# Moving the samples' state products and two key products of a decoder trunk from VectorE to GpSimd

## The chip, the core and the metric

The kernel runs on one core of one Trainium2 chip. The metric is the time of one execution on the device in microseconds (us); less is better. The engines are named as the profile names them: PE is TensorE, DVE is VectorE, ACT is ScalarE, POOL is GpSimd, and SP is SyncE, which here issues nearly all the transfers.

## The reference

Two layers of a decoder trunk run for one prompt of 256 tokens (with 16 learned meta tokens ahead of it, 272 rows) and for 8 samples of one token each; both groups share the weights. Layer 0 is RWKV-7 time mixing with 64 heads of 64, layer 1 is windowed attention on a shared K/V. All arithmetic is float32. What matters here is layer 0:

```python
def rwkv7_step(S, inp):
    r, d, k, v, kk, b = inp
    sa = jnp.einsum('bhij,bhj->bhi', S, kk)
    S = S * d[:, :, None, :] - sa[..., None] * b[:, :, None, :] + v[..., None] * k[:, :, None, :]
    return S, jnp.einsum('bhij,bhj->bhi', S, r)
...
    kk = k_h * k_k.astype(f32).reshape(hn)
    kk = kk / jnp.maximum(jnp.sqrt(jnp.sum(kk * kk, axis=-1, keepdims=True)), 1e-12)
    k_h = k_h * (1.0 + (a_h - 1.0) * k_a.astype(f32).reshape(hn))
    b_h = kk * a_h
...
    y = y + jnp.sum(r_h * k_h * r_k.astype(f32), axis=-1, keepdims=True) * v_h
    y = y.reshape(B, T, WIDTH).astype(dt) * jax.nn.silu(z)
    return y @ w_out, S_fin.astype(S0.dtype), xn[:, -1]
```

For the samples `T` is 1 and the state `S` comes in from outside: 8 x 64 heads x 64 x 64 numbers. The last addition is called the bonus below.

## The kernel before

The activations lie transposed: 128 channels (two heads) on the partitions, 280 columns beside each other (272 prompt rows, then the 8 samples). A weight tile `raw_*` of 128 x 512 is loaded by SP, ACT casts it to `whi_*` (line 195), DVE subtracts to get `wlo_*` (line 197), and PE forms each product in three parts (lines 218 to 220: high by high, low by high, high by low). A weight tile feeds 12 such matmuls. This goes on from start to end, so PE always has such a product to do if its weights are split in time.

The span has three stages. Until about 140 us the input is normalised and the first projections run. From about 140 to 1240 us `phase_a` runs (this is where the change lies): PE's order is written by hand in `drive`, which walks through the large products in pieces of six matmuls (one piece is one *position*) and lets small streams put their work between the pieces. A stream is a Python generator: `yield 5` gives the word back for five positions, and `yield 5, f` waits beyond that until `f()` holds. So a number in a `yield` is a distance on PE, while ACT, DVE and POOL get what a list scheduler of the toolchain makes of the program; each engine then runs its own list in order. After 1240 us come the output projection, the attention layer and the final projection.

The streams that the change and the prediction touch:

- `preps`: `prep(u)` for 16 pairs of channel tiles (u is 0 to 15). It loads `kT` and `rT` (keys and receptance, 128 x 2 x 280), scales `kk`, forms the factor `km` on ACT (line 902), multiplies it into `kT` in place on DVE (line 904), forms `ta` (line 906) and the running sum of the decay (line 910). POOL gathers the samples' eight columns of six tensors into `sm` (line 932); PE turns `sm` around (line 935, tile `ps_sm`), and ACT copies it out (line 937). Then the bonus: `rk` is r times r_k times k (line 945), split into `rklhi` (ACT) and `rkllo` (DVE) like a weight, and summed over a head on PE (line 954, `ps_bo`); DVE multiplies the sum into `vT` (line 955). Buffers of `km` and of `rk` share the tag "sq", which has two.
- `main`: for pairs of u (o is 0 to 7), `solve(o)` and `chain(o)`, the recurrence over five blocks of rows. Ahead of a solve stands `substitute(o)`: four POOL instructions on 128 x 256 to 128 x 320 (lines 1064 to 1067: `Noff`, two `nd`, `N`), then a DVE transpose (`NL`, line 1069), 28 small dependent DVE instructions (lines 1075 and 1077), and the transposes `TN` and `TR` (lines 1081, 1082), on which PE's `ps_so` (line 1102) waits. In the chain's fifth block POOL clears `W` (line 1198). DVE's `X<-FS` (line 1227) lets PE's next block begin (line 1191).
- `group_norm(o)`: PE transposes (`ps_yt`, line 1275), DVE scales into the bonus tile `vT` (line 1276).
- `decodes`: `decode(g)` for four groups of samples' states, each in eight pieces `dS` of 128 x 512. DVE multiplies the piece by `kk` into `dT` and sums (lines 1313, 1314), then by `ddr` (d times r) and sums. `dS` and `dT` have one buffer each, so the next piece's load waits for the last reader. The flag `self.samples` is true only while a chain runs, and a piece is let in only then.

`late_gates` waits for `('d', 3)`, the end of the fourth group, and for the last chain.

Of the kernel before, what the change touches and what calls it, by code (L numbers as in the profile page):

```python
# [12 lines left out]
F32 = mybir.dt.float32  # L13
F32R = mybir.dt.float32r
I32 = mybir.dt.int32
AF = mybir.ActivationFunctionType
ALU = mybir.AluOpType
AX = mybir.AxisListType
# [7 lines left out]
L = NM + SEQ  # L26
NS = 8
N = L + NS
# [32 lines left out]
P_W0, P_A0, P_KK, P_KA, P_RK, P_GG, P_GB = 144, 176, 208, 256, 288, 320, 352  # L61
# [48 lines left out]
class Kernel:  # L110
# [747 lines left out]
    def prep(self, u):  # L858
        nc, rp, I = self.nc, self.rp, self.I
        V, A, G = nc.vector, nc.scalar, nc.gpsimd  # L860
        tt = V.tensor_tensor
        MU, AD, SU = ALU.mult, ALU.add, ALU.subtract
        dma = nc.sync.dma_start
        p0 = 2 * u
        b, sl = p0 // 4, slice(p0 % 4, p0 % 4 + 2)
        w = lambda n, bufs=1: rp.tile([128, 2, N], F32, tag=n, bufs=bufs, name=f"{n}{u}")
# [5 lines left out]
        hi = rp.tile([128, 544], F32R, tag="lhi", name=f"lhi_{u}")[:LR, :512]  # L872
# [17 lines left out]
        kT = w("kT", 2)  # L890
        dma(kT, self.kd[b][:, sl])
        rT = w("rT")
        dma(rT, self.rd[b][:, sl])

        kk = w("kk")
# [4 lines left out]
        for j in range(2):  # L900
            km = rp.tile([128, N], F32, tag="sq", bufs=2, name=f"km{j}_{u}")
            A.activation(km, a[:, j], AF.Identity, scale=self.par2[:, 64 + p0 + j:65 + p0 + j],
                         bias=self.par2[:, 96 + p0 + j:97 + p0 + j])
            tt(kT[:, j], kT[:, j], km, op=MU)
        A.activation(a, a, AF.Identity, scale=-0.5, bias=self.half[:, 1:2])
        tt(a, a, kk, op=MU)
        A.activation(cl, cl, AF.Identity, scale=0.5, bias=self.half[:, 0:1])

        for j in range(2):
# [28 lines left out]
        g, h0 = p0 // 8, (2 * p0) % 16  # L938
# [1 line left out]
            dma(self.vecd[g][:, :, h0 + 2 * j:h0 + 2 * j + 2].rearrange("v b h j -> (v b) (h j)"),  # L940
                sr[48 * j:48 * j + 48].rearrange("p h j -> p (h j)"))

        def rk_of(j):
            rk = rp.tile([128, L], F32, tag="sq", bufs=2, name=f"rk{j}_{u}")
            V.scalar_tensor_tensor(rk, rT[:, j, :L], self.pcol(P_RK, p0 + j), kT[:, j, :L], op0=MU, op1=MU)
            self.split(two[0][:, j], two[1][:, j], rk)
        two = [rp.tile([128, 2, L], F32R, tag=n, name=f"rk{n}{u}") for n in ("lhi", "llo")]
        for j in range(2):
            rk_of(j)
        for j in range(2):  # L950
            yield 5 - j if u > 1 else 3, self.pp_free
            ps = self.pp_bank(f"ps_bo{j}_{u}")
# [329 lines left out]
    def decode(self, g):  # L1282

        nc, rp, I, O = self.nc, self.rp, self.I, self.O
        V, A, G = nc.vector, nc.scalar, nc.gpsimd
        tt = V.tensor_tensor
        MU, AD = ALU.mult, ALU.add
        dma = nc.sync.dma_start
        ve = rp.tile([128, 6, 64], F32, tag="ve", name=f"ve{g}")
        dma(ve, self.vecd[g].rearrange("v b h j -> (b h) v j"))  # L1290
        kk, bn, kp, rr, vv, dd = (ve[:, i] for i in range(6))
        gb = rp.tile([128, 3, 64], F32, tag="gb", name=f"gb{g}")
        dma(gb, I['consts'][:, C_GB + 192 * g:C_GB + 192 * g + 192].rearrange("p (v j) -> p v j", v=3))
        y = rp.tile([128, 64], F32, tag="dy", name=f"dy{g}")
        sa = rp.tile([128, 64], F32, tag="dsa", name=f"dsa{g}")
        t = rp.tile([128, 64], F32, tag="dt2", name=f"dt2{g}")
        st = rp.tile([128, 8], F32, tag="dst", name=f"dst{g}")

        dr = rp.tile([128, 64], F32, tag="ddr", name=f"ddr{g}")
        tt(dr, dd, rr, op=MU)  # L1300
        NI = 8
        rowb = lambda a: a.unsqueeze(1).to_broadcast((128, NI, 64))
        for q in range(64 // NI):
            if q:
                yield 3
            S = rp.tile([128, NI, 64], F32, tag="dS", bufs=1, name=f"dS{g}_{q}")
            T = rp.tile([128, NI, 64], F32, tag="dT", bufs=1, name=f"dT{g}_{q}")
            iq = slice(NI * q, NI * q + NI)
            dma(S.rearrange("p i j -> p (i j)"),
                I['state_wkv'][g, q])  # L1310
            yield 5 if g < 3 else 4, lambda: self.samples
            for w, o in ((kk, sa), (dr, y)):
                tt(T, S, rowb(w), op=MU)
                V.reduce_sum(o[:, iq], T, axis=AX.X)
        dma(self.sad[g], sa)
        for i, w in ((3, bn), (4, kp)):
            tt(t, w, rr, op=MU)
            V.reduce_sum(st[:, i:i + 1], t, axis=AX.X)
        V.scalar_tensor_tensor(y, sa, st[:, 3:4], y, op0=MU, op1=AD)
        V.scalar_tensor_tensor(y, vv, st[:, 4:5], y, op0=MU, op1=AD)  # L1320

        V.reduce_sum(st[:, 0:1], y, axis=AX.X)
        V.tensor_scalar(st[:, 0:1], st[:, 0:1], 1.0 / 64, None, op0=MU)
        V.tensor_scalar(y, y, st[:, 0:1], None, op0=ALU.subtract)
        V.tensor_tensor(t, y, y, op=MU)
        V.reduce_sum(st[:, 1:2], t, axis=AX.X)
        V.tensor_scalar(st[:, 1:2], st[:, 1:2], 1.0 / 64, GN_EPS, op0=MU, op1=AD)
        self.rsqrt(st[:, 1:2], rp, "d", g)
        V.scalar_tensor_tensor(y, y, st[:, 1:2], gb[:, 0], op0=MU, op1=MU)
        V.tensor_tensor(y, y, gb[:, 1], op=AD)  # L1330
        V.tensor_tensor(t, rr, kp, op=MU)
        V.tensor_tensor(t, t, gb[:, 2], op=MU)
        V.reduce_sum(st[:, 2:3], t, axis=AX.X)
        V.scalar_tensor_tensor(y, vv, st[:, 2:3], y, op0=MU, op1=AD)
        yield 16, self.pp_free
        ps = self.pp_bank(f"ps_dy{g}")
        nc.tensor.transpose(ps[:64, :128], y, self.ident)
        yt = ps[:64, :128].rearrange("p (b a q) -> p q a b", a=8, q=2)
        for q in range(2):
            A.copy(self.ys[64 * q:64 * q + 64, 8 * g:8 * g + 8], yt[:, q])  # L1340
# [632 lines left out]
```

## Time and profile before

| what | value |
|---|---|
| time, median of 3 runs | 2119.73 us (2116.61 to 2119.84) |
| the profiled execution's own time | 2118.32 us |
| its span, first to last instruction | 2116.5 us |
| mean granted PE clock | 0.990 |
| busy PE, DVE, ACT, POOL | 2064.9, 1697.8, 1263.8, 122.5 us |
| POOL instructions | 188 |
| DMA | 446.28 MB, 211 GB/s |

The busy time of an engine is the time in which it had an instruction running; a PE that is busy for 98% of the span leaves some 50 us in which it waited. A wait is put down to the instruction whose end released it. `PEclk` is the clock that TensorE was granted, as a share of full speed. In the views below a row such as `128x512 f32<-128x512 f32` gives the shapes of output and input, and numbers with an x count instructions.

### The profile page before, as it was taken

To read this page: it belongs to the slowest core of one execution; us is meant where nothing else is said; L and a number is where in the kernel's file an instruction comes from. 1 tells how busy PE (TensorE), PEld (TensorE's weight loads), DVE (VectorE), ACT (ScalarE), POOL (GpSimd) and SP (SyncE) were. 2 spreads that over 40 slices of the span, in tenths; PEclk is the share of its full clock that TensorE was granted. 3 is DMA by queue.
4 is the path that set the end of the run, shared out by engine and by line. 5 is a ranking of instruction groups with operands and counts; after the bars stand their busy time and mean duration, and the time that the engine had idled before them with its cause. 6 is when DMAs were issued, how large, how long until landed. Compare 5 with 4: busy or idle time off the path is not lost.

```text
span 2116.5 us, 55871 instructions
## 1 busy us (share of the span) xinstructions
PE 2064.9 (98%) x21420; PEld 1965.8 (93%) x21420; DVE 1697.8 (80%) x4112; ACT 1263.8 (60%) x2790; POOL 122.5 (6%) x188
## 2 busy tenths in 40 slices
PE   9999999899999999999999999999999999999997
PEld 7999899889899989899999999999999999999997
DVE  8867777687678878888888788997888888878885
ACT  3457766576766757767676445565565655544443
POOL 0011100001010010100100001100000000000000
PEclk9999999999999999999999999999999999999999
DMA  7898667658756876777657687757455444567774
GB/s 258 314 312 250 189 213 241 188 181 290 216 180 205 260 229 198 211 217 222 203 152 246 207 257 243 247 172 227 132 167 156 146 155 130 181 210 247 232 219 132
DMA packets 276356, 446.28 MB, mean 211 GB/s; under 512 B 54056, under 2 KB 97768, under 8 KB 275696
## 3 DMA queue, kind: packets, MB, share of 16 engines
q1 hardware_dynamic: 275656, 441.66, 66.6%
q8 instruction: 168, 2.75, 0.5%
q10 hardware_dynamic: 432, 1.05, 0.1%
q14 instruction: 100, 0.82, 0.1%
HBM read 381.69 MB, written 65.03 MB: 211 GB/s over the span
## 4 chain that ended last, share of the span: by engine, by line
PE 87%; DVE 5%; ACT 3%; DMA 3%; issue 2%; SPq 0%; POOL 0%; DVEq 0%; POOLq 0%; ACTq 0%
PE ps_z L218 6%; PE ps_z L219 6%; PE ps_z L220 6%; PE ps_k L218 3%; PE ps_ob L218 3%; PE ps_ob L220 3%; PE ps_v L218 3%; PE ps_ob L219 3%; PE ps_r L218 3%; PE ps_q L218 3%; PE ps_q L220 3%; PE ps_q L219 3%; PE ps_k L219 3%; PE ps_k L220 3%; PE ps_v L220 3%; PE ps_v L219 3%
## 5 line engine op out<-in xcount | busy, mean ns | idle before, releaser
L218 PE MATMUL ps_z<-mhlm,whi_z 128*128 128x280 f32 x512 | 158.6, 310 | 2.8 <-ACT sr L937 2.0
L219 PE MATMUL ps_z<-mhlm,whi_z 128*128 128x280 f32 x512 | 150.6, 294 | 0.0
L220 PE MATMUL ps_z<-mhlm,wlo_z 128*128 128x280 f32 x512 | 150.3, 294 | 0.0
L218 PE MATMUL ps_q<-bmh,whi_qb 128*128 128x264 f32 x512 | 150.0, 293 | 0.1
L218 PE MATMUL ps_z<-bmh,whi_zb 128*128 128x264 f32 x512 | 147.4, 288 | 0.0
L220 PE MATMUL ps_q<-bmh,wlo_qb 128*128 128x264 f32 x512 | 145.6, 284 | 0.6 <-DVE wlo_qb L197 0.6
L219 PE MATMUL ps_q<-bml,whi_qb 128*128 128x264 f32 x512 | 145.6, 284 | 0.0
L219 PE MATMUL ps_z<-bml,whi_zb 128*128 128x264 f32 x512 | 145.5, 284 | 0.0
L220 PE MATMUL ps_z<-bmh,wlo_zb 128*128 128x264 f32 x512 | 145.4, 284 | 0.0
L218 PE MATMUL ps_ob<-ghi,whi_ob 128*128 128x264 f32 x512 | 145.3, 285 | 0.0
L220 PE MATMUL ps_ob<-ghi,wlo_ob 128*128 128x264 f32 x512 | 144.6, 284 | 0.0
L219 PE MATMUL ps_ob<-glo,whi_ob 128*128 128x264 f32 x512 | 144.6, 283 | 0.0
L195 ACT CAST whi_ob<-raw_ob 128x512 fp32r<-128x512 f32 x128 | 79.1, 620 | 96.9 <-PE ps_ob L219 77.8
L195 ACT CAST whi_oa<-raw_oa 128x512 fp32r<-128x512 f32 x128 | 79.2, 620 | 88.0 <-PE ps_oa L219 30.6
L197 DVE TENSOR_TENSOR wlo_r<-raw_r,whi_r 128x512 fp32r<-128x512 f32 x128 | 87.8, 691 | 42.6 <-ACT whi_r L195 41.3
L218 PE MATMUL ps_v<-mhlm,whi_v 128*128 128x280 f32 x384 | 119.8, 312 | 0.4 <-ACT st L790 0.4
L218 PE MATMUL ps_k<-mhlm,whi_k 128*128 128x280 f32 x384 | 119.1, 310 | 1.0 <-ACT st L790 1.0
L195 ACT CAST whi_v<-raw_v 128x512 fp32r<-128x512 f32 x128 | 79.0, 619 | 65.8 <-PE ps_v L219 37.7
L197 DVE TENSOR_TENSOR wlo_v<-raw_v,whi_v 128x512 fp32r<-128x512 f32 x128 | 87.3, 687 | 36.9 <-ACT whi_v L195 35.6
L195 ACT CAST whi_zb<-raw_zb 128x512 fp32r<-128x512 f32 x128 | 78.2, 619 | 62.9 <-PE ps_z L219 38.5
L220 PE MATMUL ps_k<-mhlm,wlo_k 128*128 128x280 f32 x384 | 112.4, 293 | 2.1 <-issue 2.1
L219 PE MATMUL ps_v<-mhlm,whi_v 128*128 128x280 f32 x384 | 112.7, 293 | 0.0
(478 smaller groups left out, 7604.1 us busy)
## 6 DMA issues: line engine op xcount, KB each, us to landing
raw_k<-a_w_rkvz SPq DMA_DIRECT2D x128, 256.0 KB
raw_v<-a_w_rkvz SPq DMA_DIRECT2D x128, 256.0 KB
raw_r<-a_w_rkvz SPq DMA_DIRECT2D x128, 256.0 KB
raw_z<-a_w_rkvz SPq DMA_DIRECT2D x128, 256.0 KB
raw_oa<-a_w_out SPq DMA_DIRECT2D x128, 256.0 KB
raw_qb<-b_w_qz SPq DMA_DIRECT2D x128, 256.0 KB
raw_zb<-b_w_qz SPq DMA_DIRECT2D x128, 256.0 KB
raw_ob<-b_w_o SPq DMA_DIRECT2D x128, 256.0 KB
```

The source lines that it names most:

```text
L195: self.nc.scalar.copy(hi, src)
L197: return self.nc.vector.tensor_tensor(lo, src, hi.bitcast(F32), op=ALU.subtract)
L218: mm(ps, wh, xh, start=start, stop=False)
L219: mm(ps, wh, xl, start=False, stop=False)
L220: return mm(ps, wl, xh, start=False, stop=stop)
```

## The change

In `prep`, the product of `kT` and `km` goes to POOL (32 instructions of 128 x 280). The product of `rT` and `kT`, without r_k, is formed right behind it, on POOL, over all 280 columns, into two tiles `rk` (32 instructions). The factor r_k is applied later: ACT makes `rklhi` from `rk` with a scale, and DVE's subtraction becomes a scalar_tensor_tensor that multiplies by r_k and subtracts.

In `decode`, both multiplications of a piece go to POOL (64 instructions of 128 x 512), the second now in place in `dS`; the two sums stay on DVE, four positions later. So a piece now takes 3 + 5 + 4 positions where it took 3 + 5 (3 + 4 in the last group), and its last reader of `dS` is a sum. Pieces of the last group no longer wait for `self.samples`.

```diff
@@ prep
-            tt(kT[:, j], kT[:, j], km, op=MU)
+            G.tensor_tensor(kT[:, j], kT[:, j], km, op=MU)
         A.activation(a, a, AF.Identity, scale=-0.5, bias=self.half[:, 1:2])
         tt(a, a, kk, op=MU)
+        rk = [rp.tile([128, N], F32, tag="sq", bufs=2, name=f"rk{j}_{u}") for j in range(2)]
+        for j in range(2):
+            G.tensor_tensor(rk[j], rT[:, j], kT[:, j], op=MU)
...
-        def rk_of(j):
-            rk = rp.tile([128, L], F32, tag="sq", bufs=2, name=f"rk{j}_{u}")
-            V.scalar_tensor_tensor(rk, rT[:, j, :L], self.pcol(P_RK, p0 + j), kT[:, j, :L], op0=MU, op1=MU)
-            self.split(two[0][:, j], two[1][:, j], rk)
         two = [rp.tile([128, 2, L], F32R, tag=n, name=f"rk{n}{u}") for n in ("lhi", "llo")]
         for j in range(2):
-            rk_of(j)
+            hi, c = two[0][:, j], self.pcol(P_RK, p0 + j)
+            A.activation(hi, rk[j][:, :L], AF.Copy, scale=c)
+            V.scalar_tensor_tensor(two[1][:, j], rk[j][:, :L], c, hi.bitcast(F32), op0=MU, op1=SU)
@@ decode
-            yield 5 if g < 3 else 4, lambda: self.samples
-            for w, o in ((kk, sa), (dr, y)):
-                tt(T, S, rowb(w), op=MU)
-                V.reduce_sum(o[:, iq], T, axis=AX.X)
+            yield 5, lambda: g == 3 or self.samples
+            G.tensor_tensor(T, S, rowb(kk), op=MU)
+            G.tensor_tensor(S, S, rowb(dr), op=MU)
+            yield 4
+            V.reduce_sum(sa[:, iq], T, axis=AX.X)
+            V.reduce_sum(y[:, iq], S, axis=AX.X)
```

The matmuls are the same in kind and number. DVE has 128 instructions fewer and POOL 128 more; ACT has the same number. In PE's list the first difference comes behind the third solve; from there the small streams stand elsewhere among the large products: the end of the first sample group comes after the third chain's start and no longer before the third solve, and from the fifth pair on solves and chains stand 36 to 150 large matmuls earlier.

Three places show the new order. The names in the rows are the tiles named above; the number behind a name is a buffer's. First POOL's list at the first prep (u = 0), where six copies into `sm` stood behind each other. Before:

```order
L932 COPY sm_2045<-vT_2043 128x2x8
L932 COPY sm_2045<-kk_2020 128x2x8
L932 COPY sm_2045<-Pp 128x2x8
L932 COPY sm_2045<-rT_2018 128x2x8
L932 COPY sm_2045<-kT_2016 128x2x8
L932 COPY sm_2045<-ta_1738 128x2x8
```

and now:

```order
L935 COPY sm_2049<-Pp 128x2x8
L904 TENSOR_TENSOR kT_2016<-kT_2016,km_0_2025 128x280
L909 TENSOR_TENSOR rk_0_2033<-rT_2018,kT_2016 128x280
L935 COPY sm_2049<-rT_2018 128x2x8
L904 TENSOR_TENSOR kT_2016<-kT_2016,km_0_2028 128x280
L909 TENSOR_TENSOR rk_0_2034<-rT_2018,kT_2016 128x280
L935 COPY sm_2049<-ta_1738 128x2x8
L935 COPY sm_2049<-kT_2016 128x2x8
```

The four products now stand ahead of the last two copies on which PE's `ps_sm` waits.

Second, POOL's list at the first solve (o = 0), where the four instructions of `substitute` stood together. Before:

```order
L932 COPY sm_3068<-Pp 128x2x8
L1067 TENSOR_TENSOR Noff<-F,consts 128x16x16
L1064 TENSOR_TENSOR nd_2955<-F,consts 128x320
L1065 TENSOR_TENSOR nd_2956<-F,consts 128x320
L1066 TENSOR_TENSOR N_1741<-nd_2955,nd_2956 128x320
L932 COPY sm_3068<-kT_3039 128x2x8
```

and now:

```order
L1068 TENSOR_TENSOR Noff<-F,consts 128x16x16
L904 TENSOR_TENSOR kT_3039<-kT_3039,km_2_3048 128x280
L1065 TENSOR_TENSOR nd_2955<-F,consts 128x320
L1066 TENSOR_TENSOR nd_2956<-F,consts 128x320
L909 TENSOR_TENSOR rk_2_3056<-rT_3041,kT_3039 128x280
L904 TENSOR_TENSOR kT_3039<-kT_3039,km_2_3051 128x280
L1067 TENSOR_TENSOR N_1741<-nd_2955,nd_2956 128x320
L935 COPY sm_3072<-ta_2768 128x2x8
L909 TENSOR_TENSOR rk_2_3057<-rT_3041,kT_3039 128x280
```

Three products have come between `Noff` and `N`; it is the same at o = 3, 4 and 6, at o = 5 one 128 x 512 product stands ahead of `Noff`, and at o = 1, 2 and 7 none comes between.

Third, DVE's list at the sixth solve (o = 5), up to `TN` or just ahead of it; `st` and `wlo_z` belong to large products. Before:

```order
L945 SCALAR_TENSOR_TENSOR rk_12_14524<-rT_14148,par,kT_14146 128x272
L945 SCALAR_TENSOR_TENSOR rk_12_14528<-rT_14148,par,kT_14146 128x272
L1075 TENSOR_TENSOR stmp_13_13984<-NL_13946 128x52
L1079 MEMSET NL_13946 128x16 x2
L197 TENSOR_TENSOR st_2_14303<-st_2_14303,yl_14126 128x560
L197 TENSOR_TENSOR wlo_z_14_14507<-raw_z_14_14504,whi_z_14_14506 128x512
L197 TENSOR_TENSOR rkllo_14523<-rk_12_14524,rklhi_14522 128x272
L1077 TENSOR_TENSOR NL_13946<-NL_13946,stmp_13_13984 128x4x13
L197 TENSOR_TENSOR rkllo_14523<-rk_12_14528,rklhi_14522 128x272
L197 TENSOR_TENSOR wlo_z_0_14541<-raw_z_0_14538,whi_z_0_14540 128x512
L1075 TENSOR_TENSOR stmp_14_13987<-NL_13946 128x28
L197 TENSOR_TENSOR wlo_z_2_14629<-raw_z_2_14626,whi_z_2_14628 128x512
```

and now:

```order
L1076 TENSOR_TENSOR stmp_13_13814<-NL_13776 128x52
L1080 MEMSET NL_13776 128x16 x2
L197 TENSOR_TENSOR wlo_z_10_14226<-raw_z_10_14223,whi_z_10_14225 128x512
L806 SCALAR_TENSOR_TENSOR st_0_14134<-st_0_14134,yl_14049 128x2x272
L812 SCALAR_TENSOR_TENSOR st_0_14134<-ys,st_0_14134 128x2x8
L1078 TENSOR_TENSOR NL_13776<-NL_13776,stmp_13_13814 128x4x13
L1277 SCALAR_TENSOR_TENSOR vT_9977<-ps_yt_0_14177,par,vT_9977 128x272
L197 TENSOR_TENSOR wlo_z_12_14249<-raw_z_12_14246,whi_z_12_14248 128x512
L1076 TENSOR_TENSOR stmp_14_13817<-NL_13776 128x28
L197 TENSOR_TENSOR st_0_14134<-st_0_14134,yl_14049 128x560
L1078 TENSOR_TENSOR NL_13776<-NL_13776,stmp_14_13817 128x2x14
L197 TENSOR_TENSOR wlo_z_14_14272<-raw_z_14_14269,whi_z_14_14271 128x512
```

The `rk` and `rkllo` instructions no longer stand inside this stretch; between the first transpose `NL` and `TN` DVE had 71 instructions and now has 54 (at o = 0 it had 64 and has 59, at o = 6 it had 54 and has 56).

## The prediction

> **What bounds the kernel now.** I read the engine totals first, then the chain that ended last, then PE's waits, and only then the lines that the diff touches. The page has these lines:
>
> ```profile
> PE 2064.9 (98%) x21420; PEld 1965.8 (93%) x21420; DVE 1697.8 (80%) x4112; ACT 1263.8 (60%) x2790; POOL 122.5 (6%) x188
> PE 87%; DVE 5%; ACT 3%; DMA 3%; issue 2%; SPq 0%; POOL 0%; DVEq 0%; POOLq 0%; ACTq 0%
> ```
>
> PE is the bound: it runs for 98% of the span and carries 87% of the chain. The change takes no matmul away, so all that it can win lies in the time in which PE waits. POOL is nearly idle. The next view splits the stage in which the change lies (columns: us, busy PE, PEld, DVE, ACT, POOL, granted clock, DMA share, GB/s), and behind it stand PE's waits in that stage (total, times, longest):
>
> ```profile
> 140.00:1240.00 1100.00, 1066.23 (x13479) 1001.45 (x13478) 867.59 (x1962) 736.99 (x1639) 84.39 (x137) 0.99 0.69 215
> ...
> PE ps_yt L1275 <- DVE vT L1276: 8.0, 2, 6.9
> PE ps_so L1102 <- DVE TN L1081: 6.1, 2, 3.5
> ...
> PE ps_ch L1191 <- DVE X L1227: 1.1, 1, 1.1
> ```
>
> PE waits 1100.00 - 1066.23 = 33.8 us here. DVE releases 15.2 us of it in these three rows, and with a wait of 1.27 (shown below) 16.5 us. That is the most that a lighter DVE can win directly. The rest is released by ACT or by "issue". A wait also costs afterwards, as these stretches behind the waits at 257, 382 and 913 us show:
>
> ```profile
> 257.00:262.00 5.00, 5.00 (x83) 4.96 (x72) 1.12 (x2) 4.11 (x7) 0.00 (x0) 0.66 0.37 109
> 382.00:387.00 5.00, 5.00 (x22) 4.99 (x23) 2.21 (x4) 3.34 (x6) 0.00 (x0) 0.50 0.48 164
> 913.40:920.00 6.60, 6.57 (x149) 6.53 (x150) 1.76 (x4) 3.96 (x6) 0.20 (x1) 0.53 0.81 265
> ```
>
> The seventh number is the granted clock: 0.66, 0.50 and 0.53. At most (1 - 0.53) x 6.6 = 3.1 us go that way behind the wait at 913, and about 2 us behind each of the others.
>
> **What the moved instructions cost.** The first rows are what DVE gives up, the sums that stay, `rklhi` and `rkllo` and an ACT instruction with a scale; the last three are the nearest that POOL has (minimum/median/maximum in ns):
>
> ```profile
> L1313 DVE TENSOR_TENSOR dT<-dS,ve x32: 670/684/693, 292.1 to 1228.9; 128x512 f32<-128x512 f32 x32
> L1314 DVE TENSOR_REDUCE dsa<-dT x32: 657/678/687, 292.8 to 1229.7; 128x8 f32<-128x512 f32 x32
> L904 DVE TENSOR_TENSOR kT<-kT,km x32: 423/443/1121, 162.0 to 1082.3; 128x280 f32<-128x280 f32 x32
> L945 DVE SCALAR_TENSOR_TENSOR rk<-rT,par,kT x32: 481/496/502, 168.3 to 1086.5; 128x272 f32<-128x272 f32 x32
> L197 DVE TENSOR_TENSOR rkllo<-rk,rklhi x32: 418/434/458, 170.8 to 1088.9; 128x272 fp32r<-128x272 f32 x32
> L195 ACT CAST rklhi<-rk x32: 412/418/433, 168.9 to 1087.4; 128x272 fp32r<-128x272 f32 x32
> L1464 ACT ACTIVATE kvh<-hT,par x16: 523/528/531, 1289.7 to 1376.8; 128x280 fp32r<-128x280 f32 x16
> ...
> L1450 POOL TENSOR_TENSOR sqacc<-sqacc,sqa x14: 791/1050/1117, 1291.5 to 1376.0; 128x280 f32<-128x280 f32 x14
> L1066 POOL TENSOR_TENSOR N<-nd,nd x8: 872/1082/1211, 229.9 to 1138.1; 128x320 f32<-128x320 f32 x8
> L1067 POOL TENSOR_TENSOR Noff<-F,consts x8: 737/747/3049, 225.7 to 1135.1; 128x256 f32<-128x256 f32 x8
> ```
>
> DVE loses 32 x 0.443 + 32 x 0.496 + 64 x 0.684 = 73.8 us (the `ddr` product has the same median). `rkllo` becomes a scalar_tensor_tensor, some 0.06 us longer (0.50 for `rk`, of that form, against 0.434), so 2 us come back. POOL gains 64 products of 280 columns at 0.79 to 1.05 us, 51 to 67 us. No row has a POOL product of 512 columns. From 256 to 320 columns the minimum grows by (872 - 737)/64 = 2.1 ns a column, so I estimate 0.872 + 192 x 0.0021 = 1.28 us undisturbed, 82 us for 64. POOL then works some 255 to 290 us of 2116: far from full. ACT's `rklhi` with a scale is some 0.11 us longer than the cast (0.528 for `kvh` against 0.418), 32 x 0.11 = 3.5 us on an engine that is idle for 363 us of the stage: nothing.
>
> **What DVE does not get back.** Where a POOL product and a DVE instruction overlap, one or both are longer. One place where POOL's product starts first, and a DVE line of the same stretch:
>
> ```profile
> 1315.97 1.08 POOL L1450 TENSOR_TENSOR sqacc<-sqacc,sqa 128x280 f32<-128x280 f32 x1 [0.47 <-ACT sqa L1445]
> ...
> 1316.32 1.28 DVE L1376 TENSOR_TENSOR sS<-sS,sve 128x512 f32<-128x512 f32 x1
> 1317.52 0.68 DVE L1378 TENSOR_TENSOR sT<-sve 128x512 f32<-128x512 f32 x1
> ...
> L1465 DVE SCALAR_TENSOR_TENSOR kvl<-hT,par,kvh x16: 495/996/1039, 1291.8 to 1377.9; 128x280 fp32r<-128x280 f32 x16
> ```
>
> The DVE product takes 1.28 us where it takes 0.68 undisturbed, and the median `kvl`, which runs beside such POOL products, 0.996 where the shortest takes 0.495. So one POOL product of 280 columns costs DVE 0 to 0.6 us, and I take 0.3 since only part of what DVE does then has two inputs in SBUF. For 512 columns I scale by 1.28/0.79: 0 to 1.0, taken as 0.5. The sum lost is 64 x 0.3 + 64 x 0.5 = 51 us (bounds 0 and 102). DVE's net relief is 72 - 51 = 21 us of 868, with bounds of +72 and -30. It is small, so the stage's waits must be gone through one by one, where the order of the lists counts for more.
>
> [...]
>
> **Part by part, in PE's time.**
>
> *The first prep (u = 0).* Here POOL's copies release PE:
>
> ```profile
> 168.28 0.20 POOL L932 COPY sm<-rT 128x16 f32<-128x16 f32 x1 [7.53 <-DMA rT<-rd]
> 169.25 0.65 POOL L932 COPY sm<-kT 128x16 f32<-128x16 f32 x1 [0.77 <-DVE kT L904]
> 169.91 0.41 POOL L932 COPY sm<-ta 128x16 f32<-128x16 f32 x1
> ...
> 170.37 0.31 PE L935 MATMUL ps_sm<-consts,sm 128*96 128x128 f32 x1 [1.22 <-POOL sm L932]
> ...
> 177.22 0.39 PE L954 MATMUL ps_bo<-rklhi,ones 128*128 128x272 f32 x1 [1.27 <-DVE vT L955]
> ```
>
> After rT lands at 168.28, POOL now runs three of the four products and then the copies: 3 x 0.79 to 1.05 plus 0.6 to 1.26 us of copies, so `sm` is whole at 171.3 to 172.7 and not at 170.32, and PE waits 1.0 to 2.4 us more. The later wait of 1.27 shrinks, because DVE has two `rk` and a `kT` fewer ahead of it (1.4 us). Net +1.0 (-0.3 to +2.4).
>
> *The first solve (o = 0).* `N` ends at 230.9, and PE waits 3.5 us for `TN`, 25 us later:
>
> ```profile
> 229.91 0.97 POOL L1066 TENSOR_TENSOR N<-nd,nd 128x320 f32<-128x320 f32 x1
> ...
> 256.24 1.27 PE L1102 MATMUL ps_so<-TN,Noff 32*32 32x16 f32 x128 [3.50 <-DVE TN L1081]
> ```
>
> Three products between `Noff` and `N` make `N` later by 3 x 0.79 to 1.05 = 2.4 to 3.2 us. Against that DVE's stretch loses five instructions of 0.4 to 0.5 us, about 2.3. What the products still overlap adds 0 to 1. Net +0.7 (-1 to +2.5) with the lower clock behind it unchanged.
>
> *The long wait for `vT`.* DVE stands until `kk` lands, and a list of instructions runs before `vT`:
>
> ```profile
> 375.65 0.51 DVE L898 SCALAR_TENSOR_TENSOR kk<-kT,par,kk 128x280 f32<-128x280 f32 x1 [4.24 <-DMA kk<-kr]
> ...
> 381.45 0.46 DVE L1276 SCALAR_TENSOR_TENSOR vT<-ps_yt,par,vT 128x272 f32<-128x272 f32 x1
> ```
>
> Of the 6.9 us, 4.2 are that transfer, and the order there is the same after the change. Two `kT` leave (-0.9); the four POOL products may stretch what is left (0 to +2.2). Net +0.3 (-0.9 to +1.3).
>
> *The sixth solve (o = 5)* waits 2.6 us for `TN` (6.1 less 3.5). This is its stretch from `N` to `TN`:
>
> ```profile
> 884.70:913.30 28.60, 24.55 (x194) 23.65 (x192) 27.89 (x74) 17.52 (x39) 3.97 (x5) 0.99 0.71 214
> ```
>
> DVE is never free in it, and between `NL` and `TN` it now has 17 instructions of 71 fewer; at 27.89/74 = 0.38 us each that is 6 us, so the wait goes, and with it part of the 3.1 us at half clock; I take -4.0 (-5.7 to 0, if the redrawn order puts another wait in its place).
>
> *The other solves.* o = 1, 2 and 7 have no product in between; at o = 3, 4 and 6 `N` is 2.4 to 3.2 us later. Their margins, from the end of `TN` to PE's use of it, first at o = 3 and then at o = 6:
>
> ```profile
> 642.50 1.14 DVE L1081 STREAM_TRANSPOSE TN<-NL 128x512 f32<-128x512 f32 x1
> ...
> 647.46 1.27 PE L1102 MATMUL ps_so<-TN,Noff 32*32 32x16 f32 x128
> ...
> 1035.30 1.12 DVE L1081 STREAM_TRANSPOSE TN<-NL 128x512 f32<-128x512 f32 x1
> ...
> 1038.80 1.27 PE L1102 MATMUL ps_so<-TN,Noff 32*32 32x16 f32 x128
> ```
>
> At o = 3 it is 647.5 - 643.6 = 3.8 us, at o = 6 1038.8 - 1036.4 = 2.4, so up to +0.8 at o = 6 and nothing at o = 3.
>
> *The last chain.* At 1206 PE waits 1.1 us for `X<-FS`, which stands in DVE's list behind a sample product that itself waited for its transfer:
>
> ```profile
> 1205.45 0.69 DVE L1313 TENSOR_TENSOR dT<-dS,ve 128x512 f32<-128x512 f32 x1 [0.24 <-DMA dS<-state_wkv]
> 1206.18 0.29 DVE L1227 COPY X<-FS 64x256 f32<-64x256 f32 x1
> ```
>
> The product leaves DVE: -1.0 (-1.1 to 0).
>
> *The sample pieces otherwise.* 43.8 us of products leave DVE beside PE's work; no row of PE's waits names a piece, so this is worth nothing directly. Four positions more per piece make the groups later; `late_gates` needs only the last, which stands far ahead of the products' end. The load of the next piece now waits on SP for a sum four positions later, and weight loads stand behind it in SP's list. The cover is the stock of split weights: SP already waits up to 5.3 us for a weight buffer, and no row of PE's waits in this stage names a weight tile.
>
> ```profile
> SPq L211 <- DVE wlo_r L197: 67.6, 54, 5.3
> ```
>
> *Sum.* 1.0 + 0.7 + 0.3 - 4.0 + 0.8 - 1.0 = -2.2 us. The redrawn order from the third solve on moves the other 17 us of ACT's and "issue" waits by +-5. Against the profiled execution's own 2118.3 this is 2116.1; the median of the runs is 1.4 us above that execution, so 2117.5.
>
> **Rivals.**
>
> *Faster: the relief decides.* DVE gets most of the 72 us back, because the sums (0.678 us each) and one-input work lie beside POOL. Then half of the 16.5 us and the half clock behind it go: 2119.7 - 8 - 3 = 2109. For it speaks that nine tenths of DVE's waited-for time is in five places; against it that 4.2 us of the longest is a transfer.
>
> *Slower: POOL in the solve's way.* One mechanism: POOL serves products ahead of `N` and `sm`, each held up by and holding up DVE's two-input instructions. If three products of 1.05 us ahead of `N` also stretch three DVE instructions by 0.6, `TN` is 5.0 us later (one alone at the 3.05 us that `Noff` took at its longest does nearly that). It decides from 3.8 us, the margin at o = 3. Then u = 0 costs 2.4, o = 0 2.5 and `vT` 1.3; o = 3 and o = 6 wait 1.2 and 2.6, with some 2 us each at the lower clock behind them; and nothing is won at o = 5. That is +14 on 2119.7: 2134. Its weaker form, the sums blocking DVE while POOL is still at work on both products (2 x 1.28 = 2.6 us undisturbed, 3.9 us with POOL stretched by half), lies between.
>
> *Nothing moves:* PE's order covers both signs, and the waits stay where they are: 2119.7.
>
> **How the numbers follow.** A measurement here tells about 0.2%, 4.2 us, from no change: faster is under 2115.5, slower over 2124. The forecast with its own spread (2113 to 2122) and "nothing moves" have together 0.45, of which 0.08 falls below 2115.5. The faster rival has 0.28, the slower 0.27. So faster 0.36, same 0.37, slower 0.27. The predicted time is the forecast's, 2117.5; the range reaches to both rivals, short of the worst: 2106 to 2130.
>
> **What would show it.** Right: POOL at 255 to 290 us, DVE at 1697.8 - 21 = about 1677; products of 512 columns on POOL at 1.3 to 1.9 us; `ps_sm` at u = 0 waiting 2.2 to 3.6 us; `ps_so` at o = 5 without a wait; `ps_yt` at 382 still 6 to 8 us. Wrong: the 512 column products at over 2 us, DVE busier than before, a new wait of PE for `TN` at o = 3, 4 or 6, or for a weight.

## The result and the profile after

The changed kernel takes 2145.82 us (median of 4 runs, 2142.62 to 2153.9) where the kernel before takes 2119.78 (4 runs, 2116.61 to 2121.99). The ratio is 1.013, with a 95% interval of 1.0099 to 1.0161: 26 us slower. The forecast was no change (2117.5, range 2106 to 2130), so the time lies outside the range and beyond the slower rival.

The engine totals of the changed kernel, and PE's waits between 140 and 1300 us (total, times, longest):

```profile
PE 2070.8 (97%) x21420; PEld 1969.6 (92%) x21420; DVE 1699.6 (79%) x3984; ACT 1265.5 (59%) x2790; POOL 263.1 (12%) x316
...
PE ps_yt L1276 <- DVE vT L1277: 16.6, 7, 9.3
PE ps_ch L1206 <- ACT W L1197: 3.9, 3, 2.0
PE ps_o L218 <- DVE xr L785: 3.6, 2, 2.8
PE ps_so L1103 <- DVE TN L1082: 3.5, 1, 3.5
PE ps_ch L1206 <- ACT W L1201: 3.2, 2, 2.1
PE ps_o L219 <- issue: 2.6, 1, 2.6
PE ps_ch L1192 <- ACT X L1228: 2.5, 2, 1.7
```

Three things are to be seen. First, DVE is as busy as before, 1699.6 us against 1697.8, with 128 instructions fewer: nothing of the 72 us came back. Second, PE is busy 5.9 us longer with the same matmuls; most of that, by an estimate, is what the lower mean clock makes of it (0.988 against 0.990 of 2065 us is some 4 us). The span is 26.9 us longer, so 21 us of new waiting make up the rest. Third, the waits stand in other places. The wait for `vT` has doubled (8.0 to 16.6), and the chain's steps (`ps_ch`, waiting for `W` and `X`) now stand in several rows, where before no row was longer than this one:

```profile
PE ps_ch L1205 <- ACT W L1196: 1.3, 2, 0.9
```

All of PE's waits at `ps_ch` together are 13.9 us and were 3.6; those at `ps_yt` grew by 8.6 us; those at `ps_o` were nothing and are 7.2 us; `ps_so` waits 4.0 us less. POOL's busy time, 263 us, lies where it was forecast (255 to 290).

What the products cost on POOL, minimum/median/maximum in ns:

```profile
L1313 POOL TENSOR_TENSOR dT<-dS,ve x32: 1274/1402/1842, 283.2 to 1220.4; 128x512 f32<-128x512 f32 x32
L1314 POOL TENSOR_TENSOR dS<-dS,ddr x32: 1272/1607/1766, 289.8 to 1221.8; 128x512 f32<-128x512 f32 x32
L904 POOL TENSOR_TENSOR kT<-kT,km x32: 777/798/1378, 161.9 to 1079.6; 128x280 f32<-128x280 f32 x32
```

The shortest 512-column product took 1.27 us, where 1.28 was estimated for an undisturbed one. Here is what a pair of them does to the solve: the timeline of DVE and POOL at the eighth solve (start, duration):

```profile
1150.63 1.51 POOL L1313 TENSOR_TENSOR dT<-dS,ve 128x512 f32<-128x512 f32 x1 [6.79 <-DMA dS<-state_wkv]
1152.22 1.28 POOL L1314 TENSOR_TENSOR dS<-dS,ddr 128x512 f32<-128x512 f32 x1
...
1150.92 1.35 DVE L1078 TENSOR_TENSOR NL<-NL,stmp 128x100 f32<-128x100 f32 x1
1152.30 1.32 DVE L1076 TENSOR_TENSOR stmp<-NL 128x108 f32<-128x108 f32 x1
1153.66 0.27 DVE L1078 TENSOR_TENSOR NL<-NL,stmp 128x108 f32<-128x108 f32 x1
...
1157.49 0.68 DVE L1316 TENSOR_REDUCE dsa<-dT 128x8 f32<-128x512 f32 x1
1158.09 0.68 DVE L1317 TENSOR_REDUCE dy<-dS 128x8 f32<-128x512 f32 x1
...
1159.81 0.50 DVE L1277 SCALAR_TENSOR_TENSOR vT<-ps_yt,par,vT 128x272 f32<-128x272 f32 x1
1160.37 0.90 PE L1276 MATMUL ps_yt<-consts,Y 128*128 128x128 f32 x3 [4.22 <-DVE vT L1277]
```

A DVE instruction of 0.27 us takes 1.35 and ends 0.13 us behind POOL's product; the next takes 1.32 beside the second product. They lose 1.08 and 1.05 us where POOL's products had 1.22 and 1.20 us left, so what is lost here goes by POOL's product, not by DVE's own length. Of 103 DVE products (TENSOR_TENSOR) with two SBUF inputs that began more than 0.1 us inside a POOL product in this run, 102 ended behind that product's end; 83 with an input in PSUM that began inside one kept their time to 0.03 us. The two sums shown (0.68) stand behind POOL's products, so they show nothing of this; four sums of the same shape that do run beside a POOL product, at 303, 830, 1124 and 1220 us, keep 0.67 to 0.69. Two copies `X<-FS`, with one input, did not: at 450 and 705 us, begun inside a POOL product, they took 0.77 and 1.27 us where the median is 0.29. It is also the last group's piece that stands here, inside a solve, where no piece stood before.

The stretch around this place, before and then after (us, PE, PEld, DVE, ACT, POOL, clock, DMA share, GB/s):

```profile
1150.00:1300.00 150.00, 148.68 (x1768) 143.71 (x1767) 120.93 (x244) 75.09 (x136) 2.36 (x4) 1.00 0.78 248
```

```profile
1150.00:1300.00 150.00, 137.91 (x1628) 132.16 (x1628) 106.87 (x213) 67.33 (x126) 18.05 (x14) 0.94 0.71 231
```

PE waits 12.1 us in these 150 us where it waited 1.3, and the clock is 0.94 and not 1.00. So a large part of the loss stands here, but as the runs below show, not all of it has this cause.

### The profile page after: what moved, and what is told of

Its sections match the earlier page's. It is cut to its first block, busy times and chain, and to the rows that moved or that the text cites. A ratio compares the mean times of both kernels' runs of the same rounds, so it can differ in the third digit from the quotient of the medians.

```text
span 2143.4 us, 55940 instructions
## 1 busy us (share of the span) xinstructions
PE 2070.8 (97%) x21420; PEld 1969.6 (92%) x21420; DVE 1699.6 (79%) x3984; ACT 1265.5 (59%) x2790; POOL 263.1 (12%) x316
## 3 DMA queue, kind: packets, MB, share of 16 engines
q10 hardware_dynamic: 432, 1.05, 0.1%
## 4 chain that ended last, share of the span: by engine, by line
PE 52%; DVE 3%; ACT 2%; issue 1%; DMA 1%; POOL 0%; SPq 0%; POOLq 0%; DVEq 0%; ACTq 0%
PE ps_z L218 5%; PE ps_z L219 5%; PE ps_z L220 5%; PE ps_ob L218 3%; PE ps_ob L220 3%; PE ps_ob L219 3%; PE ps_q L218 3%; PE ps_q L220 3%; PE ps_q L219 3%; PE ps_o L218 2%; PE ps_oa L219 2%; PE ps_oa L218 2%; PE ps_oa L220 2%; PE ps_o L219 1%; PE ps_o L220 1%
## 5 line engine op out<-in xcount | busy, mean ns | idle before, releaser
L197 DVE TENSOR_TENSOR wlo_r<-raw_r,whi_r 128x512 fp32r<-128x512 f32 x128 | 92.5, 727 | 47.7 <-ACT whi_r L195 46.6
L197 DVE TENSOR_TENSOR wlo_oa<-raw_oa,whi_oa 128x512 fp32r<-128x512 f32 x128 | 92.0, 727 | 36.7 <-ACT whi_oa L195 35.0
```

The costliest lines, as they stand in the source:

```text
L197: return self.nc.vector.tensor_tensor(lo, src, hi.bitcast(F32), op=ALU.subtract)
```

## The experiments

Theory A said that POOL's products hold up DVE and so PE; theory B that the new `yield`s, which move the order of the work, make the waits whatever engine multiplies. All ratios are against the kernel before, run on the same chip in the same batch (its medians there were 2116.7 to 2118.2).

**e1: all products back on VectorE, the rest as changed.**

```diff
-            G.tensor_tensor(kT[:, j], kT[:, j], km, op=MU)
+            V.tensor_tensor(kT[:, j], kT[:, j], km, op=MU)
...
-            G.tensor_tensor(T, S, rowb(kk), op=MU)
+            V.tensor_tensor(T, S, rowb(kk), op=MU)
```

(`rk` and the second product likewise.)

> The changed kernel with all 128 moved products back on VectorE, in the changed positions (sums four positions later, r_k in the split); PE's order is that of the changed kernel. [...] Theory B (the new positions and PE's new order make the waits, whatever engine multiplies): it stays slow, 2136 to 2148.

2140.12 us, 1.0111 (1.009 to 1.0132). The loss stays without POOL: theory A is not the main cause.

**e2: only the sample pieces' part; e3: only the prep's part** (each the hunk of that function from the change).

> Only the sample pieces' part of the change (64 products of 128x512 on GpSimd, sums four positions later); the prep as before. PE's order is that of the changed kernel. Theory A: these products are the longer ones (1.27 us and more), so most of the loss stays: 2133 to 2142. Theory B: about the whole loss, 2138 to 2148.

2142.8 us, 1.0116 (1.0095 to 1.0137), as theory B had it.

> Only the prep's part of the change (64 products of 128x280 on GpSimd, r_k in the split); the sample pieces as before, so PE's order is that of the kernel before. Theory A: a third to a half of the loss, 2124 to 2132. Theory B: no loss, 2116 to 2123.

2123.19 us, 1.0023 (1.001 to 1.0035), between the two ranges. The prep's part costs a little (6.5 us), the pieces' part nearly all. PE's list in e1 and e2 is that of the changed kernel, in e3 that of the kernel before.

**e4: sample products on GpSimd, at the old place.**

```diff
-                tt(T, S, rowb(w), op=MU)
+                G.tensor_tensor(T, S, rowb(w), op=MU)
```

> The kernel before with the sample pieces' two multiplications on GpSimd and nothing else: each sum still stands right behind its product, PE's order is that of the kernel before, and VectorE must wait for GpSimd at each sum. [...] Theory B (order): PE's order is the old one, so near 2120, up to 2128.

2128.48 us, 1.0054 (1.0035 to 1.0072). This is half a microsecond above theory B's range. With the old list on PE, POOL costs 12 us, and that includes DVE's waits for it at the sums (20.4 us in all). It is half of what the changed yields cost without POOL.

**Which of the yields is it?** Four kernels, all with the products on VectorE. e5 keeps the sums beside their products and only changes the yields:

```diff
-            yield 5 if g < 3 else 4, lambda: self.samples
+            yield 5, lambda: g == 3 or self.samples
             for w, o in ((kk, sa), (dr, y)):
                 tt(T, S, rowb(w), op=MU)
                 V.reduce_sum(o[:, iq], T, axis=AX.X)
+            yield 4
```

e6 is e5 without `g == 3 or`; e7 is e1 without `g == 3 or`; e8 is the kernel before with `g == 3 or` and nothing else.

> The kernel before with only the yields of the sample pieces changed as in the change (5 positions, the last group let in at any time, 4 positions at the end of a piece); products and sums stay on VectorE and stand beside each other as before, so the sums are not late. PE's order is that of the changed kernel. B1 (PE's order, in which solves and chains from the third pair stand 48 to 78 large matmuls earlier) or B2 (the last group runs inside the eighth solve): as slow as the all-on-VectorE run, 2134 to 2146. B3 (the sums being four positions after their products): the loss goes, 2115 to 2124.

2135.05 us, 1.0095 (1.0074 to 1.0116).

> As the run with the sums near, but the last group is let in only while a chain runs, as before. PE's order has the solves and chains as in the changed kernel, the last group's end apart. B1: most of the loss stays, 2130 to 2142. B2: the loss goes, 2116 to 2124; in between, 2124 to 2130, both have a share.

2136.11 us, 1.0088 (1.0068 to 1.0109).

> The changed kernel with all products on VectorE (sums four positions later) and the last group let in only while a chain runs. B1: 2132 to 2142. B2: 2116 to 2126. B3: as the all-on-VectorE run, 2136 to 2144; the difference to the run before it is what the lateness of the sums and r_k's place cost.

2135.71 us, 1.0091 (1.0071 to 1.0112).

> The kernel before with one change: the pieces of the last sample group do not wait for a chain to run. Solves and chains stand where they stood before. B2: its pieces come into the eighth solve, which grows by some 10 us, and the time is 2126 to 2134. B1 and B3: 2115 to 2122.

2131.37 us, 1.0067 (1.0051 to 1.0084).

The lateness of the sums is not it (e5 is as slow as e7). Both other causes cost by themselves, and they do not add up: 18 to 19 us for the longer pieces alone, 14.6 for the free last group alone, 18 for both. In e8 the pieces do come into the eighth solve, and PE's longest wait there is for `TN`:

```profile
PE ps_so L1102 <- DVE TN L1081: 5.8, 1, 5.8
```

**How much could the pieces' products win at all?** e9 puts them on GpSimd while a piece keeps its eight positions: the sums move into the three positions that stand ahead of the next load.

```diff
             if q:
-                yield 3
+                yield 2
+                sums(*last)
+                yield 1
...
+            G.tensor_tensor(T, S, rowb(kk), op=MU)
+            G.tensor_tensor(S, S, rowb(dr), op=MU)
+            last = S, T, iq
+        yield 2
+        sums(*last)
...
-        yield 16, self.pp_free
+        yield 14, self.pp_free
```

e10 and e11 leave the products out: e10 has `for z in range(3): G.memset(T, 0.0)` in the place of each, and e11 has `V.reduce_sum(o[:, iq], S, axis=AX.X)` alone. e12 is the kernel before with a piece of seven positions (`yield 2` for `yield 3`).

> The kernel before with the sample products on GpSimd, written so that a piece still takes eight positions (the sums stand two positions after the products, inside the three that were there already, and the last group waits for a chain as before). PE's order is that of the kernel before, letter for letter. If the changed kernel loses mostly by the new period of the pieces: near the kernel before, 2114 to 2124. [...]

2124.93 us, 1.0033 (1.0019 to 1.0048), one microsecond above the stated range: 7.4 us slower, less than e4 but not nothing.

> Leaves the sample products out: where each stood, GpSimd fills the product's tile three times (it writes SBUF and reads nothing), and VectorE sums that. PE's order is that of the kernel before. VectorE still waits for GpSimd at each sum. [...]

2131.62 us, 1.0068 (1.0049 to 1.0087). That is 14 us slower, more than e4's 12, though DVE's waits for POOL at the sums are only 6.2 us, where e4 has 20.4. DVE is busy 33 us less and its other instructions are hardly stretched (2.7 us in all between 140 and 1260, against 62 in the changed kernel), so the fills do not hold it up (in the changed kernel 14 DVE instructions with two SBUF inputs began inside one of POOL's fills, and none took more than 0.01 us longer). But the fills wait for no load, so they start early and stand ahead of other work in POOL's list, and the first sum comes 17 us later than before (310 us against 293). PE's largest new row of waits, 8.5 us at `ps_r` for ACT's `st`, was not followed back, so what makes this run slow stays open, and it says nothing on the price of the waits.

> Leaves the 64 sample products out altogether (both sums read the piece itself), so VectorE has 43.8 us less to do and GpSimd nothing more. PE's order is that of the kernel before. It is the most that moving these products could ever win. If VectorE's load in the chains counts for PE: 2100 to 2112. If PE's order and the transfers set the waits: 2113 to 2120.

2111.3 us, 0.9968 (0.9955 to 0.9981). The time lies just inside the first range, so DVE's load does count for PE, but for little: without 43.8 us of DVE's work the kernel gains 6 us. With the old order of the work this is the ceiling for the samples' products. No run leaves out the prep's products.

> The kernel before with a piece of seven positions (two for three ahead of the next load), all on VectorE. The groups end sooner, and solves and chains from the third pair stand 6 to 36 large matmuls earlier. If longer groups are what costs, since their pieces reach chains that had none: not slower, 2110 to 2120. If any shift of solves and chains against the large products costs: 2124 to 2136.

2133.76 us, 1.0079 (1.006 to 1.0099). Shorter pieces cost 16 us, as longer ones do. Solves and chains move here by only 6 large matmuls, and from the sixth pair on by 36, so the cost does not go by the size of the move. That speaks against the length of a group and for something that any new period moves.

**What a new period moves: the solves.** At a group's end PE does one transpose, `ps_dy`, with a bank that all small streams share, and taking it sets `pp_pos`: the next user of such a bank waits for three positions. In the kernel before, the first group's `ps_dy` stands just ahead of a prep's `ps_bo`, which is thereby held back by 48 large matmuls (two `ps_vt`, which take such a bank too, pass ahead of it), and with it everything from the third solve on. In the changed kernel `ps_dy` comes later, that hold is gone, and from the third pair on solves and chains stand 48, and from the sixth pair on 78, large matmuls earlier; the preps between them move by up to 96. So "The change" has this wrong: the first difference in PE's list stands ahead of the third solve, at this `ps_dy`, and the solves and chains are early from the third pair on, not from the fifth. Here is PE's list by the traces, without the large products: the name, and the count of matmuls of lines 218 to 220 ahead of it:

```
before:  ps_ch@2382 ps_dy@2382 ps_vt@2400 ps_vt@2418 ps_bo@2436 ... third solve ps_so@2724
e6:      ps_ch@2382 ps_bo@2388 ps_vt@2406 ps_vt@2424 ... third solve ps_so@2676
```

So the hold can be moved by itself. In e13 and e14 `ps_dy` takes its bank without setting `pp_pos`, and the hold is set at positions given by hand:

```diff
+    HOLD = (289, 620, 844, 989)
...
                 for s in list(live):
+                    if len(streams) == 6 and s[0] is streams[4] and self.pos in self.HOLD:
+                        self.pp_pos = self.pos
...
-        ps = self.pp_bank(f"ps_dy{g}")
+        ps = self.bank(self.pp, f"ps_dy{g}")
```

These four are where `ps_dy` stood before. e13 is e6 with them. e14 is the kernel before with the positions of e6 (387, 651, 854, 1015). e15 and e16 are the whole change, on GpSimd, with the four old positions, the last group waiting for a chain (e15) or free (e16).

> As the run with the sums near and the last group let in only during a chain (2136 us, all on VectorE), with one thing more: the transpose at a group's end no longer holds back the prep behind it, and a hold is put at the four positions where it stood in the kernel before. Solves and chains so stand exactly where they stood before; the pieces stay long. Shift theory (the moved solves cost): 2116 to 2123. Piece theory (the longer groups cost): 2130 to 2140.

2126.41 us, 1.0041 (1.0026 to 1.0057), between the two ranges. In its trace every solve, chain and prep stands where it stood before. What is left is shown behind the next run.

> The kernel before with its pieces untouched, but the hold that a group's end puts on the prep moved to the positions it has in the changed yields, so that solves and chains stand 48 to 78 large matmuls earlier, as in the changed kernel. Shift theory: 2130 to 2140. Piece theory: 2115 to 2122.

2140.54 us, 1.0098 (1.0077 to 1.0119). With the old pieces, and nothing but the shift, the whole loss of the changed yields is there; in the trace solves, chains and preps stand exactly as in the changed kernel. The shift is shown to be a cause by itself. Its waits, between 140 and 1300 us:

```profile
PE ps_yt L1279 <- DVE vT L1280: 8.8, 2, 8.0
PE ps_ch L1209 <- ACT W L1200: 4.9, 3, 2.2
PE ps_ch L1195 <- DVE X L1231: 3.6, 3, 1.6
...
PE ps_ch L1209 <- ACT W L1204: 2.8, 1, 2.8
PE ps_ch L1218 <- ACT X L1214: 2.3, 2, 1.5
```

PE's waits at `ps_ch` are 15.1 us here, 3.6 before. They are 10.4 in e6, 11.2 in e12, 15.8 in e1, and 1.9 in e13, where the solves are back. Over the whole span PE is idle for 63.3 us here and 51.6 before, so they make up nearly all of the 11.7 us between; the other 6.1 us of the longer span are PE busy for longer with the same matmuls (2071.0 us against 2064.9). So the chain's steps are what the shift makes late. One such wait from e14, at the third chain, with DVE, then ACT:

```profile
591.22 0.18 DVE L295 TENSOR_SCALAR rsyk<-kx 128x35 int32<-128x35 int32 x1 [4.08 <-DMA kx<-kr]
591.31 0.43 DVE L959 TENSOR_TENSOR vT<-ps_bo,vT 128x272 f32<-128x272 f32 x1
...
591.78 0.52 ACT L960 ACTIVATE vT<-vT,par 128x272 f32<-128x272 f32 x1 [2.04 <-DVE vT L959]
592.31 0.74 ACT L1204 COPY W<-ps_ch 16x256 f32<-16x256 f32 x2
```

DVE's list has an instruction that waits 4.1 us for a transfer (`kx`, for the keys' norms), ahead of a bonus product. ACT's list has the bias of that product ahead of the chain's `W`. So `W`, which has nothing to do with either, comes late, and PE waits 2.8 us for it. The changed kernel has the same sight at 600 us: `kx` 3.38 us, then `W`, then 2.09 us of PE. The kernel before has this stall too, but there another step of the chain meets it, and PE waits 0.9 us:

```profile
587.60 0.18 DVE L295 TENSOR_SCALAR rsyk<-kx 128x35 int32<-128x35 int32 x1 [3.24 <-DMA kx<-kr]
...
588.90 0.52 ACT L956 ACTIVATE vT<-vT,par 128x272 f32<-128x272 f32 x1 [2.60 <-DVE vT L955]
589.33 0.35 ACT L1196 COPY W<-ps_ch 128x256 f32<-128x256 f32 x1
```

Not every such wait has a transfer behind it. At 948 us in e14 ACT works without a pause on a prep (`Pp`, `cl`, `km`) and a weight, and the chain's `W` stands behind that; PE waits 2.2 us:

```profile
946.11 0.67 ACT L922 ACTIVATE cl<-cl 128x560 f32<-128x560 f32 x1
...
946.76 0.62 ACT L195 CAST whi_z<-raw_z 128x512 fp32r<-128x512 f32 x1
947.28 0.62 ACT L906 ACTIVATE km<-ta,par 128x280 f32<-128x280 f32 x1
947.81 0.35 ACT L1200 COPY W<-ps_ch 128x256 f32<-128x256 f32 x1
```

The other waits at `ps_ch` were not followed one by one.

In e13, what is left stands in another place, behind 1262 us:

```profile
PE ps_oa L218 <- ACT whi_oa L195: 5.8, 1, 5.8
PE ps_oa L220 <- DVE wlo_oa L197: 1.7, 1, 1.7
PE ps_oa L218 <- ACT ghi L195: 1.7, 1, 1.7
PE ps_oa L219 <- DVE glo L197: 0.8, 1, 0.8
```

`ghi` and `glo` are made behind `late_gates`, which waits for the fourth group's end. With longer pieces that are let in only during the chain, its last sum ends at 1257 us and not at 1232, and PE waits 10 us for what follows. That is what `g == 3 or` repairs (e16 below waits 1.3 us there); e8 shows its price where the pieces are short and it was not needed.

> The whole change on GpSimd, with solves and chains put back to their old places by the same holds and the last group let in only during a chain. Shift theory: what is left is GpSimd's own cost, the 6.5 of the prep and the 7.4 of the samples: 2122 to 2132. Piece theory: 2136 to 2146.

2140.4 us, 1.0104 (1.0088 to 1.012). This lies in the piece theory's range, and the shift theory's expectation is missed. What it had left out is what e13 showed: the last group ends late (its last sum at 1271 us), and PE waits 8.9 us at `ps_oa`, with GpSimd's cost on top.

> The same with the last group free, as in the change. If that costs by itself what it cost the kernel before (14.6): 2136 to 2146. If it costs nothing beside GpSimd: 2122 to 2132.

2129.62 us, 1.0061 (1.004 to 1.0082), in the second range. With solves put back and the last group free, the change costs 11.4 us and not 26.

**Is the rest GpSimd?** e17 is e16 with all products on VectorE, e18 is e16 with the prep as before the change. PE's list is the same in all three.

> The changed kernel with solves and chains put back by the holds, the last group free, and all 128 products on VectorE; PE's list is that of the put-back run before it (2129.6 us). If GpSimd is the rest: 2116 to 2122. If the long pieces and the free last group are the rest: 2126 to 2134.

2117.17 us, 1.0001 (0.999 to 1.0011). Nothing is left: long pieces, late sums and the free last group together cost nothing once the solves stand at their old places. (Taken singly two of them do: long pieces without the free last group cost 8 us in e13, the free last group with short pieces 14.6 us in e8.)

> The same with the sample products on GpSimd and the prep as before the change, on VectorE. If the prep's products carry 6.5 us as they did alone: 2120 to 2126. If the samples' products or the pieces carry the rest: 2126 to 2133.

2122.75 us, 1.0034 (1.0019 to 1.0049), in the first range.

So the loss is laid out by steps: the sample products on GpSimd cost 0.34% (5 to 7 us), the prep's products there bring it to 0.61% (some 6 us more, as alone in e3; the two intervals overlap), and the shift of solves and chains, caused by the changed period of a piece, takes it to 1.3% (15 us more). The steps go by their order and do not simply add: with the solves shifted, GpSimd adds only 0.2% (e1 at 1.0111, the changed kernel at 1.013), which is within the intervals. PE's waits in e17 at the chain are small again (1.6 us in all), as the rows between 140 and 1300 show:

```profile
PE ps_yt L1280 <- DVE vT L1281: 10.2, 4, 6.7
PE ps_so L1107 <- DVE TN L1086: 5.8, 3, 2.7
...
PE ps_ch L1196 <- ACT X L1232: 0.9, 2, 0.7
```

With the products on GpSimd in the same order (e16), PE waits again, at `ps_yt` above all. The first rows are e16's, the last is that of e3, where the prep's products alone are moved; before it was 8.0 us in two places:

```profile
PE ps_yt L1280 <- DVE vT L1281: 16.2, 6, 8.4
PE ps_ch L1219 <- ACT X L1215: 3.4, 2, 2.5
...
PE ps_yt L1276 <- DVE vT L1277: 15.0, 6, 8.8
```

No version beat the kernel before: the best, e17, equals it, and where GpSimd multiplies the samples' states in the old order (e4, e9, e18) the kernel loses 5 to 12 us, while leaving those products out wins 6.

## Why the prediction was wrong

**The step that failed** is the last term of the sum, "the redrawn order from the third solve on moves the other 17 us of ACT's and "issue" waits by +-5". The redrawing was seen in the lists, though put too late (behind the third solve), but was taken as a spread around nothing. It costs 15 us here and 21 to 22 alone (e14), because PE waits for the chain's short steps (`ps_ch` 15.1 us for 3.6), which in the waits that were followed had come to stand behind other streams' work on DVE and ACT. It lies in no rival either: the slower rival and its weaker form were both about POOL.

**The sum by parts**, -2.2 us for products that move to POOL, failed too. Its own measurement is e16, where solves and chains stand as before (and e17, the same on VectorE, costs nothing): +11.4 us, more than the upper bounds of its parts together (2.4 + 2.5 + 1.3 + 0 + 0.8 + 0 = 7.0). It went through the waits that PE already had, and put all places without a wait at nothing. In e16 PE waits for `vT` in six places (16.2 us) where it waited in two (8.0), and 7.3 us at `ps_ch` for 3.6.

**DVE's net relief** was taken as 21 us, between +72 and -30; it measured -2. The stretch of DVE's common instructions between 140 and 1260 us came to 62 us where 51 was estimated for all, and it includes short instructions: `stmp` and `NL` of 0.27 us at 1.35. (By summed durations DVE has 9.4 us less; in the busy time, where overlapping ends count once, it has 1.8 us more.) That POOL's products hold up DVE's was right (102 of 103 above), and so was taking only a part of DVE's work as held, though not every overlap makes one of the two longer: the 83 with an input in PSUM kept their time. The mean was low, and the conclusion (relief is small) held. The faster rival counted on the sums and on one-input work beside POOL: the four sums kept their time, the two copies of `X` did not.

**The first prep**: +1.0 predicted. `ps_sm` waits 1.4 us for 1.2, and the 1.27 us wait for `vT` at 177 is gone, so it is a gain of about 1 us; e3 has both changes too. **The first solve**: +0.7 predicted, 3.5 us as before. **The long wait for `vT`** was to grow by 0.3 and at most 1.3; it grew by 2.4, from 6.9 to 9.3. The first four rows are from before, the others from now:

```profile
376.60 1.33 DVE L910 TENSOR_TENSOR_SCAN cl<-reset,cl 128x272 f32<-128x272 f32 x2
...
378.29 0.68 DVE L197 TENSOR_TENSOR wlo_v<-raw_v,whi_v 128x512 fp32r<-128x512 f32 x1
378.89 0.44 DVE L904 TENSOR_TENSOR kT<-kT,km 128x280 f32<-128x280 f32 x1
379.25 0.73 DVE L906 TENSOR_TENSOR ta<-ta,kk 128x560 f32<-128x560 f32 x1
...
377.04 0.51 DVE L898 SCALAR_TENSOR_TENSOR kk<-kT,par,kk 128x280 f32<-128x280 f32 x1 [5.04 <-DMA kk<-kr]
...
377.99 2.44 DVE L913 TENSOR_TENSOR_SCAN cl<-reset,cl 128x272 f32<-128x272 f32 x2
...
380.44 1.27 DVE L197 TENSOR_TENSOR wlo_v<-raw_v,whi_v 128x512 fp32r<-128x512 f32 x1
381.62 1.31 DVE L906 TENSOR_TENSOR ta<-ta,kk 128x560 f32<-128x560 f32 x1
...
384.43 0.45 DVE L1277 SCALAR_TENSOR_TENSOR vT<-ps_yt,par,vT 128x272 f32<-128x272 f32 x1
```

The transfer took 0.8 us longer. Beside POOL's products the two scans took 2.44 us for 1.33, and the two instructions of 0.7 us 0.6 more each: 2.3 us in all, against 0.9 that the two `kT` gave back. So the stretch reached the upper end (2.2), where I had taken about half.

**The sixth solve**: PE no longer waits for `TN` there, but 0.4 us for its next step at 923. The number came out, by luck: the 2.6 us wait is gone in e14 too, where DVE keeps all its work and only the order moves (PE waits 2.1 us at the solve's next step instead), and with the old order and POOL's products 1.3 us of it stay in e3 and 2.0 in e16. So it was the shift that took it away, and fewer DVE instructions alone take about half of it at most. **The last chain**: `X`'s wait at 1206 is gone, as predicted, and so it is in e9 and e11, which have the old order. **The sample pieces otherwise** were set at nothing. Their products are worth little indeed (e11: 6 us at most), but three things were overlooked: that the group's end carries the hold that places the solves; that `late_gates`, with longer pieces behind the flag, no longer has its group's end far ahead (10 us of waits in e13); and that a last group free of the flag runs inside the eighth solve. There `TN` came 26 us behind `N` where it took 18; but it took as long in e17, where PE waits only 0.8 us for it, so this alone is not the loss.

**The slower rival** (2134, products ahead of `N` at o = 3 and 6) named the right sign for a wrong reason: PE waits for `TN` at the first solve alone, 3.5 us as before. Its time lay outside the stated range, which ended at 2130 though this rival had a chance of 0.27. With solves and chains at their old places, moving products to POOL cost 5 to 7 us in e3, e9 and e18, and 12 in e4.

## What to carry to other kernels

Where a hand-written order counts in positions, changing the length of one stream moves all streams that share a resource with it, and that can cost more than the moved work could win. Two moves of the order were tried here (e12, e14) and both cost; that every move would is not shown. Before an edit is judged, the old order can be put back by force (here, a hold at four positions) and the edit measured by itself: 1.0001 without the engine, 1.0061 with it, 1.013 with the shift. And the ceiling can be measured first, by leaving the work out: for the samples' products it was 6 us for 43.8 us of DVE's time, less than what the shift alone cost.

## What the runs showed of the hardware

In the changed kernel, of 103 DVE products with two SBUF inputs that began more than 0.1 us inside a GpSimd product, 102 ended behind that product's end: 0.27 us became 1.35 beside a product of 1.51 us. The 83 with an input in PSUM kept their time to 0.03 us, four sums kept 0.67 to 0.69 us, and two copies with one input took 0.77 and 1.27 us for 0.29. GpSimd fills of the samples' tiles, 192 of them at 0.53 us (e10), stretched DVE by 2.7 us in all between 140 and 1260 us. Longer waits of PE went with a longer busy time for the same matmuls: 21 us more of waiting with 5.9 more of busy time (the changed kernel), 11.7 with 6.1 (e14).
